# The order of the passes in products with stationary weights

## The chip, the cores and the metric

The kernel runs on one core of a Trainium2 chip. The metric is the device time of one execution in microseconds (us), the median over several runs. The core's TensorE multiplies a stationary operand of 128 x 128, loaded by one instruction (a weight load), with a moving operand of up to 512 columns that streams through it in another (a matmul, here called a pass). Sums are kept in PSUM, eight banks of 512 float32 columns per partition. VectorE (DVE), ScalarE (ACT) and GpSimd (POOL) do the elementwise work, and SyncE (SP) issues the loads.

## The reference

Two blocks run one after the other on 256 tokens of width 2048. The first has an even layer (short convolution, a state-space part, memory attention) and an odd layer (latent attention, memory attention), the second a retention layer and an MLP. Nearly all arithmetic lies in products of activations with large weights:

```python
def even_layer(x, mem_n, norm_w, w_in, ...):
    h = rms_norm(x, norm_w)
    proj = h @ w_in
    sc_b, sc_c, sc_v, sc_z, ssd_z, ssd_xbc, ssd_dt, mq, mz = _split(proj, EVEN_SPLITS)
    ...
    return x + jnp.concatenate([y_a, y_b, y_m], axis=-1) @ w_out

def odd_layer(x, mem_n, positions, norm_w, w_in, ...):
    h = rms_norm(x, norm_w)
    proj = h @ w_in
    c_q, c_kv, k_r, z_c, mq, mz = _split(proj, ODD_SPLITS)
    ...
    return x + jnp.concatenate([y_c, y_m], axis=-1) @ w_out

def squared_relu_mlp(h, w_up, w_down):
    return jnp.square(jax.nn.relu(h @ w_up)) @ w_down
```

The retention layer has the same form: an input product that gives queries, keys, values and gates, and an output product.

## The kernel before

Each product is cut into jobs. A job is one block of output columns of one weight, summed over the whole inner dimension in tiles of 128 (k tiles). PLAN lists the jobs in the order in which they run. A job is worked off in pieces of one to four k tiles (subs). For each piece SyncE loads float32 weights into a `raw` tile. ScalarE rounds them to a high part and VectorE computes the low part (value minus high part); both lie in one tile called `w` (`split_to`, `emit_split`, line 187 and line 165 in the profile). Activations are kept in the same two parts. One product of values becomes three products of parts: high by high, high by low, low by high. `emit_mm` issues them; every matmul goes through the helper `mm`, so that all have line 180. The sums of a job stand in a PSUM tile `g` of two banks; there are two such tiles.

`run_stream` sets the order by hand: for each piece it issues the splits up to two pieces ahead, the loads beyond them, then the piece's matmuls, and then steps the waiting tasks (evacuation of finished jobs, transposes, attention, normalisation), whose small matmuls fall between two pieces.

There are three kinds of jobs:

- **Kind A** (`lay_a`): the weights are stationary and the activations move, so the output is transposed. A job covers 256 output columns as two neighbouring tiles of 128, with tile 0 in bank 0 and tile 1 in bank 1. For each tile and k tile there are two passes. The first has the high weights stationary and 512 moving columns: the high and the low part of 256 tokens side by side. The second has the low weights stationary and 256 moving columns: the high part of the tokens. The profile calls them `g<-h,w` and `g<-mem,w`. Line 287 later adds the two halves of the bank.
- **Kind A3** (`lay_uq`, `lay_ukv`): weights stationary, three passes of 256 columns into one region (`g<-cq,w`, `g<-ck,w`).
- **Kind B** (`lay_b`): the activations are stationary and up to 512 weight columns move; three passes for the first 128 tokens into bank 0, then three for the second 128 into bank 1 (`g<-w,h`, `g<-w,y`, `g<-w,yr`, `g<-w,hid`, `g<-w,mem`).

PLAN holds 100 jobs of kind A. Each has 16 k tiles and two tiles: 3,200 pairs of one 512-column and one 256-column pass.

Of the kernel before, what the change touches and what calls it, by code (L numbers as in the profile page):

```python
# [118 lines left out]
def block_kernel(ctx, tc, a, out):  # L119
# [14 lines left out]
    def nm(s):  # L134
        serial[0] += 1
        return f"{s}_{serial[0]}"
# [42 lines left out]
    def mm(o, l, r, start, stop=True):  # L179
        nc.tensor.matmul(o, l, r, start=start, stop=stop, skip_group_check=True)  # L180
# [171 lines left out]
    def emit_mm(m, only=None):  # L352
        s = subs[m]
        job = s.job
        if s.first and job.ps is None:
            job.ps = psg.tile([128, 2, 512], F32, tag="g", name=nm("g"))
        hv_, lv_ = splits[m]
        for k in range(s.n):
            kt = s.k0 + s.s0 + k
            xh, xl, xb = job.x.hi(kt), job.x.lo(kt), job.x.both(kt)  # L360
            for kind, dst, (c0, c1), bk, t in job.layout(job.ps):
                if only is not None and t != only:
                    continue
                wh, wl = hv_[:, k, c0:c1], lv_[:, k, c0:c1]
                if kind == "A":
                    trio = ((dst, wh, xb), (dst[:, 0:256], wl, xh))
                elif kind == "A3":
                    trio = ((dst, wh, xh), (dst, wh, xl), (dst, wl, xh))
                else:
                    sh, sl = xh[:, t * 128:t * 128 + 128], xl[:, t * 128:t * 128 + 128]  # L370
                    trio = ((dst, sh, wh), (dst, sh, wl), (dst, sl, wh))
                for d, l, r in trio:
                    mm(d, l, r, start=bk not in job.started, stop=False)
                    job.started.add(bk)

    def spawn(gen):
        tasks.append(gen)
# [8 lines left out]
    def run_stream():  # L386
# [15 lines left out]
        for m, s in enumerate(subs):  # L402
            if s.first and s.job.key in hooks:
                hooks[s.job.key]()
            while at["split"] < n and at["split"] <= m + (min(AHEAD, m) if m < n - 4 else 3):
                dma_to(at["split"])
                emit_split(at["split"])
                at["split"] += 1
            dma_to(max(min(at["split"] + 3, m + 3), 6))
            drive(lambda: all(k in s.job.x.done for k in range(s.k0 + s.s0, s.k0 + s.s0 + s.n)))  # L410
            if m < n - 2:
                emit_mm(m)
                del splits[m]
                if s.last:
                    spawn(s.job.post(s.job.ps))
                step_tasks()

        for t in range(2):
            for m in (n - 2, n - 1):
                emit_mm(m, only=t)  # L420
            final_rows(subs[-1].job.ps, t)
# [1007 lines left out]
    for entry in PLAN:  # L1429
        key = entry[0]  # L1430
        kind, rest = key[0], key[1:]
# [115 lines left out]
```

## Time and profile before

| | |
|---|---|
| median of 3 runs | 2640.96 us (2640.96 to 2641.23) |
| the profiled execution's own time | 2640.79 us |
| its span, first to last instruction | 2639.0 us |
| PE (matmuls) busy | 2621.6 us, 99% of the span, 14,160 passes |
| PEld (weight loads) busy | 2272.8 us, 86%, 14,160 loads |
| DVE, ACT, POOL busy | 62%, 49%, 5% |
| TensorE's granted clock, mean | 0.999 |

Busy time is the time in which at least one instruction of an engine runs by its record. Matmul records overlap each other, so the busy share of PE says that it was never idle, and not how fast it went. How fast is read from how many passes fall into a stretch. A window's count includes each pass of which any part lies in it.

### The profile page before, as it was taken

The numbers are of one execution on the slowest core, as the hardware profiler recorded it, in microseconds if no ns is written. First come the engines' busy times: TensorE is split into PE (matmuls) and PEld (weight loads), VectorE is DVE, ScalarE is ACT, GpSimd is POOL, SyncE is SP. The second block draws the span as 40 slices with busy tenths as digits, with TensorE's granted clock in tenths as the row PEclk, the third lists the DMA queues.
The fourth block names the chain that finished last, engine by engine and source line by source line (L and its number), as shares of the span: only waits on it lengthen the run. The fifth ranks groups of instructions, "written<-read, shape, count | busy, mean of one in ns | idle before, by whom it ended". The sixth has DMA issues, their size and how long they took to land.

```text
span 2639.0 us, 34784 instructions
## 1 busy us (share of the span) xinstructions
PE 2621.6 (99%) x14160; PEld 2272.8 (86%) x14160; DVE 1643.1 (62%) x2067; ACT 1298.8 (49%) x1772; POOL 140.6 (5%) x104
## 2 busy tenths in 40 slices
PE   9999999999999999999999999999999999999998
PEld 7998888888899999888888888888888888888886
DVE  7657787656545887657565556565656545555554
ACT  6566555544445675545444444444455434534543
POOL 4100232000000000000000000000000000000000
PEclk9999999999999999999999999999999999999999
DMA  7454444565545434455444554554555555555553
GB/s 278 169 192 170 160 160 160 192 219 198 185 156 197 159 138 180 176 191 215 179 176 182 190 195 179 180 198 173 189 186 195 195 192 189 191 193 190 191 209 142
DMA packets 74833, 488.87 MB, mean 185 GB/s; under 512 B 8880, under 2 KB 10672, under 8 KB 20656
## 3 DMA queue, kind: packets, MB, share of 16 engines
q1 hardware_dynamic: 74096, 486.11, 51.2%
q8 instruction: 111, 1.82, 0.3%
q10 hardware_dynamic: 576, 0.53, 0.1%
q14 instruction: 50, 0.41, 0.0%
HBM read 484.51 MB, written 2.10 MB: 184 GB/s over the span
## 4 chain that ended last, share of the span: by engine, by line
PE 96%; DVE 1%; ACT 1%; DMA 1%; POOL 1%; issue 0%; POOLq 0%; ACTq 0%; DVEq 0%; SPq 0%
PE g L180 91%; PE tr L436 1%; PE ro L180 1%; PE at.s L180 1%; DVE w L165 0%; PE rs L180 0%; ACT w L187 0%; POOL xsq L487 0%; DMA raw<-in_mem_v_dram 0%; PE at.o L180 0%; PE yd L180 0%; DMA raw<-in_mem_k_dram 0%; PE seg L180 0%; DVE xbc L174 0%; PE ma.o L180 0%
## 5 line engine op out<-in xcount | busy, mean ns | idle before, releaser
L165 DVE TENSOR_TENSOR w<-raw,w 128x1024 fp32r<-128x1024 f32 (+4 forms) x929 | 1116.4, 1212 | 818.8 <-ACT w L187 817.2
L187 ACT CAST w<-raw 128x1024 fp32r<-128x1024 f32 (+4 forms) x929 | 936.3, 1026 | 652.0 <-PE g L180 639.9
L180 PE MATMUL g<-h,w 128*128 128x512 f32 (+1 forms) x6144 | 1077.5, 336 | 1.0 <-DVE qx L165 1.0
L180 PEld LDWEIGHTS g<-h,w 128*128 128x128 f32 x6144 | 935.0, 188 | 125.6 <-issue 2.0
L180 PE MATMUL g<-w,h 128*128 128x512 f32 (+3 forms) x2208 | 460.8, 368 | 0.0
L180 PEld LDWEIGHTS g<-w,h 128*128 128x128 f32 x2208 | 391.9, 188 | 59.4
L180 PE MATMUL g<-w,hid 128*128 128x512 f32 x1536 | 349.0, 389 | 0.8 <-DVE x L174 0.8
L180 PEld LDWEIGHTS g<-w,hid 128*128 128x128 f32 x1536 | 288.1, 188 | 61.0 <-DVE x L174 1.3
L180 PE MATMUL g<-w,y 128*128 128x512 f32 x1152 | 264.5, 390 | 0.0
L180 PEld LDWEIGHTS g<-w,y 128*128 128x128 f32 x1152 | 215.2, 188 | 44.7 <-ACT y L187 0.4
L287 ACT COPY low<-g 128x512 f32<-128x512 f32 x100 | 58.6, 586 | 337.0 <-PE g L180 337.0
L180 PE MATMUL g<-w,yr 128*128 128x512 f32 x768 | 176.2, 390 | 0.0
L180 PEld LDWEIGHTS g<-w,yr 128*128 128x128 f32 x768 | 143.7, 188 | 29.6
L165 DVE TENSOR_TENSOR x<-x,g 128x512 f32<-128x512 f32 x48 | 30.8, 684 | 68.0 <-PE g L180 68.0
L165 DVE TENSOR_TENSOR blk<-g,low 128x512 f32<-128x512 f32 x100 | 68.3, 683 | 0.4 <-PE g L180 0.4
L1327 POOL TENSOR_TENSOR s<-s,om 128x1 f32<-128x1 f32 x16 | 22.6, 1411 | 598.6 <-DVE s L169 598.6
L180 PE MATMUL g<-cq,w 128*128 128x256 f32 x432 | 54.3, 282 | 0.0
L465 POOL TENSOR_TENSOR stat<-s,om 128x2 f32<-128x2 f32 x7 | 10.0, 1435 | 820.9 <-DVE s L171 820.9
L180 PEld LDWEIGHTS g<-cq,w 128*128 128x128 f32 x432 | 52.1, 189 | 0.1
L180 PE MATMUL g<-w,mem 128*128 128x512 f32 x192 | 46.7, 397 | 2.6 <-ACT w L187 0.8
L180 PEld LDWEIGHTS g<-w,mem 128*128 128x128 f32 x192 | 35.2, 188 | 13.1 <-DVE mem L174 3.0
L177 ACT ACT_TABLE_LOAD x28 | 35.9, 1283 | 20.4 <-PE pre L180 10.4
(267 smaller groups left out, 1461.0 us busy)
## 6 DMA issues: line engine op xcount, KB each, us to landing
raw<-in_w_in_dram SPq DMA_DIRECT2D x96, 1024.0 KB, 4.8
raw<-in_ret_w_in_dram SPq DMA_DIRECT2D x96, 1024.0 KB, 4.8
raw<-in_mlp_w_up_dram SPq DMA_DIRECT2D x64, 1024.0 KB, 4.8
raw<-in_mlp_w_down_dram SPq DMA_DIRECT2D x64, 1024.0 KB, 4.8
raw<-in_w_out_dram SPq DMA_DIRECT2D x48, 1024.0 KB, 4.8
raw<-in_ret_w_out_dram SPq DMA_DIRECT2D x32, 1024.0 KB, 4.8
raw<-in_w_in_dram SPq DMA_DIRECT2D x12, 704.0 KB, 4.0
raw<-in_mem_k_dram SPq DMA_DIRECT2D x8, 1024.0 KB, 4.9
```

What stands on the lines that cost most here:

```text
L165: nc.vector.tensor_tensor(o, x, y, op)
L177: nc.scalar.activation(o, x, f, **kw)
L180: nc.tensor.matmul(o, l, r, start=start, stop=stop, skip_group_check=True)
L187: nc.scalar.copy(hi, x)
L287: nc.scalar.copy(low, ps[:, :, 256:512])
L436: nc.tensor.transpose(ps[:, i, t * 128:(t + 1) * 128], src(t, kp + i), ident)
L465: nc.gpsimd.tensor_tensor(dst, v, mhalf[:, 0:ncols], ALU.pow)
L1327: nc.gpsimd.tensor_tensor(r, vv, mhalf[:, 0:1], ALU.pow)
```

## The change

Within one k tile of a job of kind A, the four passes were issued tile by tile: 512 columns and 256 columns of tile 0, then 512 and 256 columns of tile 1. Now both 512-column passes come first (tile 0, tile 1) and then both 256-column passes (tile 0, tile 1). The instructions are the same in number and operands; only their order differs, and that of the weight loads with them: high 0, low 0, high 1, low 1 becomes high 0, high 1, low 0, low 1. Consecutive passes now go to different banks. Kinds A3 and B keep their order.

```diff
@@ emit_mm
             xh, xl, xb = job.x.hi(kt), job.x.lo(kt), job.x.both(kt)
+            groups = []
             for kind, dst, (c0, c1), bk, t in job.layout(job.ps):
...
-                for d, l, r in trio:
-                    mm(d, l, r, start=bk not in job.started, stop=False)
-                    job.started.add(bk)
+                groups.append((kind, bk, trio))
+            order = []
+            while groups:
+                pair = [groups.pop(0)]
+                if pair[0][0] == "A" and groups and groups[0][0] == "A" and groups[0][1] != pair[0][1]:
+                    pair.append(groups.pop(0))
+                for i in range(max(len(g[2]) for g in pair)):
+                    order += [(g[1], g[2][i]) for g in pair if i < len(g[2])]
+            for bk, (d, l, r) in order:
+                mm(d, l, r, start=bk not in job.started, stop=False)
+                job.started.add(bk)
```

## Rows read from the trace of the kernel before

**Rows 1.** The page: the span, the engines' busy time, the clock in 40 slices.
```profile
span 2639.0 us, 34784 instructions
...
PE 2621.6 (99%) x14160; PEld 2272.8 (86%) x14160; DVE 1643.1 (62%) x2067; ACT 1298.8 (49%) x1772; POOL 140.6 (5%) x104
...
PEclk9999999999999999999999999999999999999999
```

**Rows 2.** The page: the chain that ended last, by engine and line.
```profile
PE 96%; DVE 1%; ACT 1%; DMA 1%; POOL 1%; issue 0%; POOLq 0%; ACTq 0%; DVEq 0%; SPq 0%
PE g L180 91%; PE tr L436 1%; PE ro L180 1%; PE at.s L180 1%; DVE w L165 0%; PE rs L180 0%; ACT w L187 0%; POOL xsq L487 0%; DMA raw<-in_mem_v_dram 0%; PE at.o L180 0%; PE yd L180 0%; DMA raw<-in_mem_k_dram 0%; PE seg L180 0%; DVE xbc L174 0%; PE ma.o L180 0%
```

**Rows 3.** Matmul groups by shape, whole span: count, busy us, mean ns of one.
```profile
L180 PE MATMUL g<-h,w 128*128 128x512 f32 x3072 | 1066.7, 392 | 1.0 <-DVE qx L165 1.0
L180 PE MATMUL g<-h,w 128*128 128x256 f32 x3072 | 856.2, 279 | 0.0
...
L180 PE MATMUL g<-mem,w 128*128 128x512 f32 x128 | 44.5, 393 | 0.0
L180 PE MATMUL g<-mem,w 128*128 128x256 f32 x128 | 35.7, 279 | 0.0
```

**Rows 4.** PE on tile g by stretch: length, busy (count of passes), clock, DMA share, GB/s.
```profile
502.00:588.00 86.00, 86.00 (x497) 1.00 0.58 202
1351.00:1371.00 20.00, 20.00 (x119) 1.00 0.51 189
1524.00:1556.00 32.00, 32.00 (x186) 1.00 0.51 189
1708.00:1738.00 30.00, 30.00 (x175) 1.00 0.49 177
1935.00:2055.00 120.00, 120.00 (x708) 1.00 0.53 187
2195.00:2295.00 100.00, 100.00 (x579) 1.00 0.53 189
2421.00:2517.00 96.00, 96.00 (x555) 1.00 0.55 196
2065.00:2185.00 120.00, 120.00 (x531) 1.00 0.56 200
```

**Rows 5.** Matmul groups by shape, 1935 to 2055 us.
```profile
L180 PE MATMUL g<-h,w 128*128 128x512 f32 x354 | 120.4, 389 | 0.0
L180 PE MATMUL g<-h,w 128*128 128x256 f32 x354 | 97.7, 276 | 0.0
```

**Rows 6.** The same, 2195 to 2295 us.
```profile
L180 PE MATMUL g<-h,w 128*128 128x512 f32 x290 | 100.6, 392 | 0.0
L180 PE MATMUL g<-h,w 128*128 128x256 f32 x289 | 80.9, 280 | 0.0
```

**Rows 7.** The same, 2065 to 2185 us (a chain of 512-column passes of kind B).
```profile
L180 PE MATMUL g<-w,hid 128*128 128x512 f32 x531 | 120.5, 389 | 0.0
```

**Rows 8.** The same, 854.1 to 858.2 us (a chain of 256-column passes of kind A3).
```profile
L180 PE MATMUL g<-cq,w 128*128 128x256 f32 x37 | 4.5, 281 | 0.0
```

**Rows 9.** The same, 169.05 to 169.5 us (256-column passes of memory attention).
```profile
L180 PE MATMUL ma.s<-mkp,mqp 128*128 128x256 f32 x5 | 0.8, 283 | 0.0
```

**Rows 10.** The same, 2189.45 to 2189.75 us (first passes of kind A behind a chain of B).
```profile
L180 PE MATMUL g<-h,w 128*128 128x512 f32 x2 | 0.7, 394 | 0.0
L180 PE MATMUL g<-h,w 128*128 128x256 f32 x1 | 0.3, 283 | 0.0
```

**Rows 11.** Weight loads of kind A, whole span: mean ns of one.
```profile
L180 PEld LDWEIGHTS g<-h,w 128*128 128x128 f32 x6144 | 935.0, 188 | 125.6 <-issue 2.0
```

**Rows 12.** What PE waited for, longest first: us in total, times, longest.
```profile
PE ma.t L545 <- DVE p L169: 1.4, 1, 1.4
PE fs L180 <- POOL xsq L495: 1.3, 1, 1.3
```

**Rows 13.** All engines by stretch: PE, PEld, DVE, ACT, POOL; clock, DMA share, GB/s.
```profile
1935.00:2055.00 120.00, 120.00 (x708) 106.13 (x707) 71.47 (x75) 61.15 (x71) 1.60 (x1) 1.00 0.53 187
2195.00:2295.00 100.00, 100.00 (x579) 88.09 (x578) 57.23 (x57) 49.73 (x58) 0.00 (x0) 1.00 0.53 189
```

## The prediction

> **What bounds the kernel now.** I began with the page [rows 1]: PE is busy for 2621.6 of 2639.0 us, in every slice, at full granted clock. The chain that ended last says the same by another way: 96% of it is PE, 91% matmuls into the tile g [rows 2]. The longest wait of a matmul is 1.4 us in total [rows 12]. So PE is never short of work, and a change of order can act only through the rate at which passes follow each other. What matters is the distance from the start of one pass to the start of the next, which the duration of a pass does not give directly, as records overlap.
>
> I read that distance from counts per stretch [rows 4]. A pass is some 390 ns long, so about two more are counted than begin in a window. In 2065 to 2185 us, only 512-column passes of kind B, 529 begin in 120 us: 226.8 ns each. Their record lasts 389 ns [rows 7], so record minus distance is 162.2 ns. In 1935 to 2055 us, only pairs of kind A, 706 passes begin in 120 us: 339.9 ns a pair. In 2195 to 2295 us, the same instructions, 577 begin in 100 us: 346.6 ns a pair. The same code thus runs at two rates, each steady over long stretches, with the same clock; I call them the short and the long rhythm.
>
> The mean durations say where the 7 ns are [rows 5, 6]: 389 and 276 ns against 392 and 280 ns. In the short rhythm the 512-column pass takes 226.8 ns, as in the chain of B, and the 256-column pass 339.9 − 226.8 = 113.1 ns; record minus distance is then 276 − 113.1 = 162.9 ns. In the long rhythm both passes take 3 to 4 ns more. Two passes that differ by 256 columns differ by 113.7 ns here, so the columns themselves cost 0.444 ns each at most, and every pass has a fixed part that comes with the change of weights. How much of that part shows depends on how a weight load (188 ns by its record, [rows 11], started during the pass before) falls against the running pass. That last is an inference; the two rates are read.
>
> How often is each rhythm there? The undisturbed windows of kind A [rows 4] hold 140 us of the short one (1351 to 1371, 1935 to 2055) and 344 us of the long one (the five others at 347). That is 412 and 993 pairs, 29% of them in the short rhythm, and a mean of 344.7 ns a pair. Over all 3,200 pairs, with the small matmuls of other tasks in between, the groups give (392 − 162.2) + (279 − 162.9) = 345.9 ns [rows 3], 1,107 us or 42% of the span. The 1.2 ns of difference are interruptions, which the change leaves where they are.
>
> **The change, part by part.** Nothing is removed or added: 6,400 passes and 6,400 loads of kind A stay, kinds A3 and B are issued as before, and no DMA, no split and no queue is touched. Within a piece only the order differs, so the same semaphores are waited for. The low weights are needed by the third pass rather than by the second, about 0.1 us later; they were not late (no wait above 1.4 us), so this is worth nothing. The bank of tile 0 gets its last pass one pass later than before, and the evacuation waits for the whole job anyway.
>
> What changes is the neighbourhood of each pass. Four passes (a quartet) were 512, 256, 512, 256 and become 512, 512, 256, 256. There are 1,600 quartets. Before, one took 2 × 344.7 = 689.4 ns undisturbed. The new one has two transitions that the trace shows only in chains of equal passes:
>
> - 512 after 512 with new weights: 226.8 ns [rows 7].
> - 256 after 256 with new weights: in the chain of A3, 281 − 162.9 = 118.1 ns [rows 8]; in memory attention, 283 − 162.9 = 120.1 ns [rows 9].
>
> The transitions 512 to 256 and 256 to 512 inside a steady pattern are known only from the old order, in its two rhythms. I price each pass by the chain of its own kind: 2 × 226.8 + 2 × 118.1 = 689.8 ns. Against 689.4 that is 0.4 ns more, times 1,600 quartets 0.6 us. The profiled execution took 2640.79 us on its own clock (its span and 1.8 us around it), 0.17 us below the median of the three runs, so the sum gives 2641.4 us, and 2641.6 beside the median.
>
> The bounds come from the nearest rows. Lowest: the new order settles wholly in the short rhythm, each 512 at 226.8 and each 256 at 113.1, 679.8 ns a quartet: 9.6 × 1,600 = 15.4 us less. Highest of all steady patterns: 256 at the 120.1 of memory attention, 693.8 ns: 4.4 × 1,600 = 7.0 us more. I take the chain of A3 between them, because its weights come from the same tile with the same offsets as those of kind A. Above both lies the first moment after a change of pattern: the first passes of kind A behind a chain of B take 394 and 283 ns [rows 10], 231.8 and 120.1 by distance. If the new order never got beyond that, a quartet would be 703.8 ns, 23.0 us more.
>
> The other engines neither gain nor stop this: in stretches of kind A, DVE is busy 57 to 60% and ACT 50 to 51%, DMA 53% [rows 13], so that they could feed a PE that is 1.4% quicker there.
>
> One rule of the Trainium skill bears on the sum. The row first: a load lasts 188 ns by its record, and starts during the pass before [rows 11]. "TensorE: Matmul & The Clock Gate" (Part 2, the steps) states that the next weights are loaded while the current pass streams, into a background buffer, in a time that goes with the columns of the weights, by its figure 128 / 1.2 = 107 ns. By that rule each pass hides one load in either order and a quartet costs the same: the sum would be zero, by my rows 0.6 us.
>
> A second rule speaks against the change. The row first: the clock is full in all 40 slices, in kind B too, where the bank changes after every third pass, and in kind A, where it changes after every second [rows 1]. The same page ("A second HAM failure mode") states that cycling through PSUM banks each iteration made PE idle briefly, so often that its clock fell between its two levels; by that rule the new order, which changes bank with every pass, could lose clock in 42% of the span. What it would cost is the fourth rival below.
>
> **The rivals.** 0.2% of the time, 5.3 us, is about what a measurement of this kernel can tell from no change; that is 3.3 ns a quartet.
>
> - *The new order locks into the short rhythm* (faster). For it: there the 512 already takes its chain's 226.8, and a 256 can take 113.1 [rows 5]. Against it: no chain of 256-column passes in the trace runs below 118.1 [rows 8, 9]. Wholly in it: 2640.8 − 15.4 = 2625.4 us; it counts as faster when a quartet comes below 686.1 ns, that is when at least one of the two 256-column passes gets most of the 5 ns.
> - *Two short passes in a row find the load late* (slower). A 512-column pass leaves the following load ample time, a 256-column pass hardly any. In the old order no short pass followed another; in the new one it happens in each quartet, and a lead won under the long passes may be spent by the first short one. Place: the second 256 and the 512 behind it. Price: 120.1 ns for each short pass [rows 9], or the long rhythm throughout, 2 × 346.6 = 693.2: 6.1 to 7.0 us more, 2647 to 2648 us. It decides from 692.7 ns a quartet. For it: the chains of short passes come no nearer to 113.1 than 118.1 [rows 8], and 71% of the undisturbed pairs are in the long rhythm already. Against it: the old mean is so near this end that little is left to lose.
> - *The pattern never settles* (slower). Changing the neighbour every second pass keeps each pass in the condition of the first ones after a boundary [rows 10]: up to 2664 us. Against it: the old order changes its neighbour with every pass and settles all the same [rows 4].
> - *The clock falls* in stretches of kind A. At half of it each of the 768 columns of a pair would cost another 0.444 ns at most: up to 341 ns × 3,200, about 1.1 ms. Against it stands every slice of the clock row; chance 1%.
>
> That the change does not do what it says can be left out: the order of issue is written out by hand.
>
> **How the numbers follow.** No measurable change 0.43 (quartet between 686.1 and 692.7 ns, the chain prices or a mixture of the rhythms like before); short rhythm for the larger part 0.25; short passes late 0.22; never settled 0.09; clock 0.01. So faster 0.25, same 0.43, slower 0.32. The time is that of the likeliest, 2641.6 us. The range must reach into both neighbours: down to 2627, nearly the short rhythm throughout, and up to 2652, beyond the highest steady pattern by a fifth of the unsettled one. Left out are most of the unsettled cases, the clock, and the last us or two of the short rhythm, together some 0.1 to 0.15. The likeliest case's own range is 2636 to 2647.
>
> **What would show it right or wrong.** In the changed kernel the counts in long stretches of kind A give the quartet: 100 us hold 580 passes at 689.8 ns, 588 at 679.8, 577 at 693.8. The records of 512 columns should be 389 ns on average, those of 256 columns 281. A mean of 276 for the short ones is the lock into the short rhythm; 283 is the late load; 392 and more for the long ones is the pattern that does not settle. The stretch of kind B, 226.8 ns a pass, must be the same, the clock row full, and the waits of PE no longer than 1.4 us. The prediction is wrong if the time moves by more than 5.3 us, and its reasoning is wrong, even at an unchanged time, if the two rhythms come at quite different prices.

## The result and the profile after

The changed kernel takes 2661.61 us (median of 4 runs, 2661.38 to 2663.26) against 2641.10 us before: 20.5 us slower, ratio 1.008, 95% interval 1.0067 to 1.0092. Executions of one kernel lay within 1.9 us of each other, the noise by which the single runs below are to be read. The forecast of 2641.6 us and its range up to 2652 were wrong. The time is that of the rival which had been given 9%, "the pattern never settles", up to 2664 us. Whether its reason was right as well is what the experiments had to tell.

The page of the changed kernel, its span, the engines and the clock, answers to [rows 1]:

```profile
span 2660.0 us, 34784 instructions
...
PE 2642.9 (99%) x14160; PEld 2280.4 (86%) x14160; DVE 1644.1 (62%) x2067; ACT 1299.2 (49%) x1772; POOL 139.5 (5%) x104
...
PEclk9999999999999999999999999999999999999999
```

The span grew by 21.0 us, PE's busy time by 21.3; the clock is full in every slice, the counts are the same. What PE waited for, longest first (us in total, times, longest), answers to [rows 12]:

```profile
PE fs L180 <- POOL xsq L504: 1.5, 1, 1.5
PE ma.t L554 <- DVE p L169: 1.2, 1, 1.2
```

No wait has appeared: the longest is 1.5 us where it was 1.4. Where did 20.5 us go? The matmul groups by shape over the whole span answer to [rows 3]:

```profile
L180 PE MATMUL g<-h,w 128*128 128x512 f32 x3072 | 970.4, 397 | 1.0 <-DVE qx L165 1.0
L180 PE MATMUL g<-h,w 128*128 128x256 f32 x3072 | 610.8, 281 | 0.0
```

The busy column invites a wrong reading: it fell from 1066.7 to 970.4 and from 856.2 to 610.8 us, and yet the kernel is slower. Passes of one shape now follow each other, their records overlap, and overlapped time counts once. The mean of one is the column to read: 392 became 397 ns for the long passes, 279 became 281 for the short ones. Times 3,200 each that is 16 and 6 us, 22 us with both rounded to whole nanoseconds.

Counts of PE on tile g by stretch (length, busy, count, clock, DMA share, GB/s), two stretches of kind A and then one of kind B, answer to [rows 4]:

```profile
1960.00:2060.00 100.00, 100.00 (x572) 1.00 0.53 187
2215.00:2315.00 100.00, 100.00 (x572) 1.00 0.51 182
2085.00:2185.00 100.00, 100.00 (x443) 1.00 0.55 195
```

570 passes begin in 100 us, in the first stretch (which had the short rhythm before) as in the second (which had the long one). A quartet takes 400 / 570 us = 701.8 ns on average in both. Against the undisturbed mean of 689.4 ns before, that is 12.4 ns × 1,600 = 19.8 us: nearly the whole loss lies between passes of kind A. The trace also records the start of every single pass, which the views here only average. Added up from each start to the next, the passes of kind A took 1110.6 us before and take 1131.1 us now, 20.5 of the 21.0 us by which the span grew. The chain of kind B has 441 passes in 100 us, 226.8 ns each, as before. In the second stretch of kind A the groups of kind A are, against [rows 6]:

```profile
L180 PE MATMUL g<-h,w 128*128 128x512 f32 x286 | 90.2, 396 | 0.0
L180 PE MATMUL g<-h,w 128*128 128x256 f32 x286 | 56.9, 280 | 0.0
```

With the same subtraction as in the prediction: 396 − 162.2 = 233.8 ns for a long pass, 280 − 162.9 = 117.1 ns for a short one; 2 × (233.8 + 117.1) = 701.8 ns, the count's own number. Most of the loss lies in the long passes: of the 20.5 us by the starts, 16.7 are theirs and 3.8 those of the short ones.

### The profile page after: what moved, and what is told of

Read it like the earlier page. It is cut to its first block, busy times and chain, and to the rows that moved or that the text cites. A ratio compares the mean times of both kernels' runs of the same rounds, so it can differ in the third digit from the quotient of the medians.

```text
span 2660.0 us, 34784 instructions
## 1 busy us (share of the span) xinstructions
PE 2642.9 (99%) x14160; PEld 2280.4 (86%) x14160; DVE 1644.1 (62%) x2067; ACT 1299.2 (49%) x1772; POOL 139.5 (5%) x104
## 4 chain that ended last, share of the span: by engine, by line
PE 96%; DVE 1%; ACT 1%; DMA 1%; POOL 1%; issue 0%; POOLq 0%; ACTq 0%; DVEq 0%; SPq 0%
PE g L180 91%; PE tr L445 1%; PE ro L180 1%; PE at.s L180 1%; DVE w L165 0%; PE rs L180 0%; ACT w L187 0%; DMA raw<-in_mem_v_dram 0%; PE at.o L180 0%; DMA raw<-in_mem_k_dram 0%; PE yd L180 0%; POOL xsq L496 0%; PE seg L180 0%; DVE xbc L174 0%; DMA mem<-in_mem_dram 0%
## 5 line engine op out<-in xcount | busy, mean ns | idle before, releaser
L180 PE MATMUL g<-h,w 128*128 128x512 f32 (+1 forms) x6144 | 1097.1, 339 | 1.0 <-DVE qx L165 1.0
L180 PEld LDWEIGHTS g<-h,w 128*128 128x128 f32 x6144 | 946.9, 188 | 143.4 <-issue 2.1
```

## The experiments

Three theories stood at the start. Theory 1: the order of lengths costs the time (what the surviving rival said). Theory 2: a pass into another bank than the one before it costs more. Theory 3: high weights loaded after high and low after low cost the time. The kernel before, run on the same chip beside each set, took 2640.8 to 2641.7 us. Each experiment was run once, unless an interval is given.

**Banks.** The first run alternates the lengths as before and lets the second tile's short pass come early; the four passes go to banks 0, 1, 1, 0.

```diff
+            if groups[0][0] == "A":
+                (_, b0, p0), (_, b1, p1) = groups
+                order = [(b0, p0[0]), (b1, p1[1]), (b1, p1[0]), (b0, p0[1])]
...
```

> The order of passes is 512 columns into bank 0, 256 into bank 1, 512 into bank 1, 256 into bank 0. Long and short passes alternate as before the change; the bank changes at two of four passes, and never between the pair of one tile's passes as it did; the high and low weights alternate too. Theory 1 (the order of lengths costs the time): 2641 us, within 8 us, since long and short alternate. Theory 2 (a pass that goes to another bank than the pass before it costs more): about half of the loss or more, 2650 to 2662 us. Theory 3 (high weights loaded after high, low after low, cost the time): 2641 us, since they alternate.

Measured: 2640.81 us. Theory 2 has no support, though the number of bank changes is that of before. The second run settles it: the lengths of the changed kernel, all four passes into one bank.

```diff
+        quads = {}
...
+                if kind == "A":
+                    quads.setdefault((k // 2, bk), []).append(trio)
+                    continue
...
+        for (_, bk), two in quads.items():
+            for i in range(2):
+                for trio in two:
+                    mm(*trio[i], start=bk not in job.started, stop=False)
+                    job.started.add(bk)
```

> Two k tiles of one tile are taken together: 512, 512, 256, 256 columns, all four into one bank, then the same for the other tile. Lengths in the order of the changed kernel, bank changes only once in four passes. Theory 1 (order of lengths): 2661 us, a quartet of about 702 ns with long passes at 233 to 236. Theory 2 (banks): 2641 us or less. Theory 3 (high after high, low after low): 2661 us.

Measured: 2662.78 us. Its groups over the whole span:

```profile
L180 PE MATMUL g<-h,w 128*128 128x512 f32 x3072 | 971.2, 397 | 1.0 <-DVE qx L165 1.0
L180 PE MATMUL g<-h,w 128*128 128x256 f32 x3072 | 611.6, 281 | 0.0
```

397 and 281 ns, as in the changed kernel, with a quarter of its bank changes. Theory 2 falls.

**Lengths against loads.** Which weights a pass loads and how many columns it has can be separated: two runs cross the two orders. In both, the second and the third pass of a quartet multiply by each other's weights, so the work is the same and the result is not.

```diff
# lengths and banks of before, loads of the changed kernel
+                seq = [(b0, p0[0]), (b0, p0[1]), (b1, p1[0]), (b1, p1[1])]
+                ws = [p0[0][1], p1[0][1], p0[1][1], p1[1][1]]
# lengths and banks of the changed kernel, loads of before
+                seq = [(b0, p0[0]), (b1, p1[0]), (b0, p0[1]), (b1, p1[1])]
+                ws = [p0[0][1], p0[1][1], p1[0][1], p1[1][1]]
# both
+                order = [(bk, (p[0], l, p[2])) for (bk, p), l in zip(seq, ws)]
```

> Lengths and banks of the kernel before (512, 256, 512, 256; bank 0, 0, 1, 1), but the stationary weights in the order of the changed kernel (high 0, high 1, low 0, low 1), so that the second and the third pass multiply with the wrong weights: a part of the products is changed, the amount of work is not. Theory 1 (order of lengths): 2641 us, within 8 us. Theory 2 (banks): 2641 us. Theory 3 (order of the loads): 2661 us.

> Lengths and banks of the changed kernel (512, 512, 256, 256; bank 0, 1, 0, 1), but the stationary weights in the order of before (high 0, low 0, high 1, low 1), so that the second and the third pass multiply with the wrong weights: a part of the products is changed, the amount of work is not. Theory 1 (order of lengths): 2661 us. Theory 2 (banks): 2661 us. Theory 3 (order of the loads): 2641 us, within 8 us.

| | loads high, low, high, low | loads high, high, low, low |
|---|---|---|
| lengths 512, 256, 512, 256 | 2640.9 us (before) | 2658.24 us |
| lengths 512, 512, 256, 256 | 2664.60 us | 2661.61 us (changed) |

The groups of the first (upper right) and of the second (lower left), whole span:

```profile
L180 PE MATMUL g<-h,w 128*128 128x512 f32 x3072 | 1083.1, 395 | 1.0 <-DVE qx L165 1.0
L180 PE MATMUL g<-h,w 128*128 128x256 f32 x3072 | 864.0, 281 | 0.0
```

```profile
L180 PE MATMUL g<-h,w 128*128 128x512 f32 x3072 | 967.5, 396 | 1.0 <-DVE qx L165 1.0
L180 PE MATMUL g<-h,w 128*128 128x256 f32 x3072 | 614.9, 281 | 0.0
```

Theories 1 and 3 both fall, each by one corner: restoring the loads does not help while the lengths are new, and restoring the lengths does not while the loads are new. In both runs the long passes last 395 to 396 ns and the short ones 281, against 392 and 279. Only one of the four corners is quick. Nor is it that the lengths change too often. A run with all eight long passes of a piece first and then all eight short ones:

```diff
+        long, short = [], []
...
+                if kind == "A":
+                    long.append((bk, trio[0]))
+                    short.append((bk, trio[1]))
+                    continue
...
+        for bk, (d, l, r) in long + short:
+            mm(d, l, r, start=bk not in job.started, stop=False)
+            job.started.add(bk)
```

> All eight long passes of a piece of four k tiles run first, then all eight short ones, at the offsets of before. Theory 1, in the form that a change of length costs the long passes after it: 1,600 quartets have one change from short to long each, here every fourth has one, so that a quarter to a half of the loss is left, 2646 to 2652 us. Theory 4: long passes now have high loads under them, short passes low loads, as in the changed kernel, and the loss stays: 2655 us or more.

Measured: 2664.74 us. Its groups over the whole span:

```profile
L180 PE MATMUL g<-h,w 128*128 128x512 f32 x3072 | 784.4, 397 | 1.0 <-DVE qx L165 1.0
L180 PE MATMUL g<-h,w 128*128 128x256 f32 x3072 | 425.6, 281 | 0.0
```

With one change from long to short in sixteen passes, the long passes are as slow as with one in four.

**Where the loads start.** What the four corners share is the tile w: its high parts start at float32 element 1048 and its low parts at 12, that is 8 and 12 beyond a multiple of 16. Theory 4: the distance between passes depends on where the data of the next load start, so that an order and the starts have to fit each other. The edit is one line in each case; the passes of kind A3 use the same tile and move with it.

```diff
-PHASES = {"A": (1024 + 24, 12), "B": (1024 + 8, 8)}
+PHASES = {"A": (1024 + 32, 0), "B": (1024 + 8, 8)}
```

> The order of the kernel before; in the tile w of kind A the high parts start at element 1056 and the low parts at element 0, both at a multiple of 16 elements, where they started at 1048 and 12 (8 and 12 beyond such a multiple). Theory 4 (the time between passes depends on where the start of the next load lies, so that order and offsets have to fit each other): the time moves by more than 8 us, most likely up towards 2655 to 2665 us. Theory 1 (the order of lengths alone): 2641 us.

> The order of the changed kernel with the same aligned starts, 1056 and 0. With equal starts the order of high and low loads can make no difference, only the order of lengths can. Theory 4: within 4 us of the old order with aligned starts. Theory 1: 20 us above the old order with aligned starts, near 2661 us.

Measured: 2653.59 us for the old order, 2648.74 us for the new one. The old order lost 12 us and the new one gained 13; with equal starts, the new order is the quicker of the two by 4.9 us, where Theory 4 had said within 4. Counts of the new order (first fence) and of the old one (second), aligned, in two stretches of kind A:

```profile
1960.00:2050.00 90.00, 90.00 (x522) 1.00 0.53 187
2220.00:2300.00 80.00, 80.00 (x464) 1.00 0.52 187
```

```profile
1960.00:2050.00 90.00, 90.00 (x517) 1.00 0.53 189
2220.00:2300.00 80.00, 80.00 (x464) 1.00 0.55 194
```

By (count − 2) per length, a quartet of the new order takes 692.3 and 692.6 ns, one of the old order 699.0 and 692.6 ns. The old order shows its short rhythm in neither stretch: one runs at 699.0 ns, a rate that it did not have in these stretches at 8 and 12. The other, and the new order in both, run at about the rate of the old long rhythm (2 × 346.6 = 693.2 ns). That the rates move with the starts is Theory 4, and Theory 1 falls a second time: it had no reason for either move.

Is it the difference of the two starts (4a), or the place of each (4b)?

> The order of the changed kernel, high and low parts both starting 8 elements beyond a multiple of 16 (1048 and 8). Theory 4a (only the difference of the two starts matters, equal starts are good for this order): 2648.7 us, within 2 us, as with both starts at a multiple. Theory 4b (the place of each start against the moving columns matters by itself): more than 4 us away from 2648.7.

> The order of the changed kernel, high parts at a multiple of 16 elements (1040), low parts 8 elements beyond one (8). Theory 4a: the difference of 8 is larger than the 4 of the changed kernel, so 2661 us or more. Theory 4b: no sign is given; a time below 2648.7 would show that unequal starts can be the better ones in this order too.

> The order of the changed kernel, high parts 8 elements beyond a multiple of 16 (1048), low parts at a multiple (0). Theory 4a: the same as with 0 and 8, within 3 us, 2661 us or more. Theory 4b: differs from it by more than 4 us.

> The order of the kernel before, both starts 8 elements beyond a multiple of 16 (1048 and 8). Theory 4a: 2653.6 us, within 2 us, as with both at a multiple. Theory 4b: more than 4 us away from that.

Measured: 2676.83, 2662.32, 2656.41 and 2643.14 us. Both starts at 8 instead of 0 cost the new order 28 us more and the old one 10 us less, with no difference between the two starts in either case. 4a had its number for 0 and 8 (2661 us or more) and missed the other three. So the place of the starts matters, and not only their difference: 4b. That it is their place against the moving columns is not shown, as those were never moved. The groups of the new order with both at 8, whole span, and the counts of the old order with both at 8:

```profile
L180 PE MATMUL g<-h,w 128*128 128x512 f32 x3072 | 977.3, 398 | 1.0 <-DVE qx L165 1.0
L180 PE MATMUL g<-h,w 128*128 128x256 f32 x3072 | 623.0, 283 | 0.0
```

```profile
1960.00:2050.00 90.00, 90.00 (x516) 1.00 0.53 189
2220.00:2300.00 80.00, 80.00 (x473) 1.00 0.53 185
```

The old order shows its two rhythms here as well, 350.2 and 339.7 ns a pair, with the stretches exchanged against [rows 4].

The starts of single passes show what the counts average. In ns from each start to the next, in order of issue (for the old order, where long and short alternate, both of a kind are alike):

| order, starts of high and low parts | 512 columns | 256 columns | quartet |
|---|---|---|---|
| old, 8 and 12, 1935 to 2055 us | 227 | 113 | 680 |
| old, 8 and 12, 2195 to 2295 us | 229 | 117.6 | 693.3 |
| new, 8 and 12, 1960 to 2060 us | 230 to 236, 231 to 236 | 113 to 118, 117 to 120 | 697 to 707 in turn, mean 702.2 |
| new, 0 and 0, 1960 to 2050 us | 231, 229 | 118, 115 | 693.3 |
| new, 8 and 8, 2220 to 2300 us | 238, 233 | 124, 118 | 713.3 |

In four of these rows each quartet is like the last within a nanosecond or so: the pattern has settled. In the changed kernel it has not: the quartets go round (707, 697, 703, 706, 698, 702 and so on).

**Does the new order have starts that suit it?**

> The order of the changed kernel, both starts 12 elements beyond a multiple of 16 (1052 and 12). Theory 5a (the new order, too, has starts that suit it, and they can be found): one of the four runs of this set comes to 2641 us or below. Theory 5b (the new order keeps a loss at any starts): all four stay at or above 2646 us. If the time goes smoothly with the start, this one lies between 2648.7 (0) and 2676.8 (8).

> The order of the changed kernel, both starts 4 elements beyond a multiple of 16 (1044 and 4). Theories 5a and 5b as in the run with 12 and 12; if the time goes smoothly with the start, between 2648.7 and 2676.8 us.

> The order of the changed kernel, high parts at a multiple of 16 (1040), low parts 12 beyond one (12), as before. Against the changed kernel only the start of the high parts differs. If the high parts' start carries the loss, near 2648.7 us; if the low parts' does, near 2661 us.

> The order of the changed kernel, high parts at a multiple of 16 (1040), low parts 4 beyond one (4). If the high parts' start carries the loss, near 2648.7 us; if the low parts' does, somewhere between that and 2662 us.

Measured: 2667.82, 2658.44, 2663.64 and 2653.47 us. None reaches 2646, so 5b stands as far as it was tried. The times with 12 and 12 and with 4 and 4 lie between 2648.7 and 2676.8, as a smooth course would have it. With the high parts at 0, the low start at 0, 4, 8 and 12 gives 2648.7, 2653.5, 2662.3 and 2663.6 us; low at 12, the high start at 0, 8 and 12 gives 2663.6, 2661.6 and 2667.8. Up to here the low start carries the larger part. But with the low start at 8, moving the high one from 0 to 8 takes the time from 2662.3 to 2676.8 us, so neither part carries the loss alone.

One more pair, the two starts of before exchanged, was tried with the new order:

> The order of the changed kernel with the two offsets exchanged: the high parts start 12 elements beyond a multiple of 16 (element 1052), the low parts 8 beyond one (element 24). Theory 4: the time moves by more than 4 us from 2661 us, either way. Theory 1: 2661 us.

It took 9412.66 us, because the granted clock fell after 740 us (last section); as a time it says nothing. Up to there the clock was full. Its groups in 520 to 570 us:

```profile
L180 PE MATMUL g<-h,w 128*128 128x512 f32 x143 | 45.0, 395 | 0.0
L180 PE MATMUL g<-h,w 128*128 128x256 f32 x143 | 28.7, 282 | 0.0
```

2 × (395 − 162.2 + 282 − 162.9) = 703.8 ns a quartet, 2 ns from the changed kernel's 701.8. Times 1,600 that would be 3 us, below the 4 us that Theory 4 had wanted to see. A change of start can happen to cost next to nothing.

**Is there a quicker version near the old one?** These two were run several times, 4 and 10, beside the kernel before:

> The order of the kernel before, high parts starting 8 elements beyond a multiple of 16 (1048), low parts 10 beyond one (10), between the two known times of 2643.1 (8 and 8) and 2641 us (8 and 12). Theory 6a (the old order changes slowly with the low start): 2640 to 2644 us. Theory 6b (each start has its own rhythms): outside of that, and if below 2636 us, a version that beats both kernels.

> The order of the kernel before, both starts 12 elements beyond a multiple of 16 (1052 and 12); against the kernel before only the high parts' start differs. Theory 6a: within 4 us of 2641 us. Theory 6b: outside of that.

Measured: 2657.08 us (ratio 1.0061, interval 1.0044 to 1.0078) and 2647.66 us (1.0025, 1.0016 to 1.0034). Both are slower than before, so 6b, but no version beats both kernels. Of the five pairs tried with the old order, 8 and 12 is the lowest, 8 and 8 lies 2 us above it, about the spread of runs, and 8 and 10, between the two, costs 14 to 16 us more than they do.

## Why the prediction was wrong

- **What bounds the kernel** was right: PE's rate between passes and nothing else. No new wait, no other engine and no clock appears in the profile after, the chain of kind B kept its 226.8 ns, and outside kind A the span grew by only 0.5 us.
- **The step that failed** is "I price each pass by the chain of its own kind: 2 × 226.8 + 2 × 118.1 = 689.8 ns". The term 2 × 118.1 was right within 2 ns (2 × 117.1). The term 2 × 226.8 was mis-sized: the long passes take 2 × 233.8. That is 14.0 ns a quartet, 22.4 us in all, of which the short ones give 3.2 us back. The chain of B has other operands: there the weights are the moving side and the activations are loaded, from other starts. The experiments show that the distance between the passes of kind A depends on where the loads' data start: the same new order goes from 2648.7 to 2676.8 us by the starts alone. A price read beside other loads did not carry over. Why the chain of B has just 226.8 ns was not tested.
- **The fixed part of a pass**, said to come with the change of weights, does not follow from 226.8 and 113.1 ns: that is 0.443 and 0.442 ns a column, which leaves nothing over. (With the 118.1 ns of the A3 chain for the short pass, 9 ns would be left.) The mean of 344.7 ns a pair took the rate of one long window for all five, whose counts give 347.1; nothing hangs on it, since the single starts of all undisturbed pairs give 344.6.
- **"The highest of all steady patterns"**, 693.8 ns, failed with the price. It was the highest among the patterns in the trace, not a bound of the chip. A quartet takes 701.8 ns on average here, and a steady one takes 713.3 with both starts at 8.
- **The rival that never settles** had the right size, since it took both prices, 231.8 and 120.1 ns, from passes of kind A behind passes of kind B [rows 10], the only rows with a long pass of kind A right after another long pass. Its sign, long records of 392 ns and more, came too (397). Its reason was only half right. By the single starts the old order does settle behind that boundary, its long passes going 233, 234, 231 and then 229 ns, and the changed kernel's quartets do not come to one length. But that is not what costs the time: with both starts at 8 the new order is settled and slower still (713.3 ns), at 0 it is settled and quick (693.3), and with eight equal passes in a row the loss stayed.
- **The late load behind short passes** did not come at its price: 117.1 ns on average, under both chains' prices. In the place that it named, the second short pass takes 118.6 ns against 115.8 for the first, and the long pass behind it 233.4, less than the next one's 234.5.
- **Lock into the short rhythm**: no stretch of the changed kernel runs in it, 572 passes in both.
- **The two rules.** Banks: the clock row is full after the change too, and four passes in one bank cost as much as four in alternating banks (2662.8 and 2661.6 us). What the Trainium skill states in "TensorE: Matmul & The Clock Gate" (A second HAM failure mode) had no bearing here. Hidden loads: if each pass hid its load at no cost in either order, as the prediction took the rule, a quartet would have kept its 689.4 ns. It takes 701.8, and moving nothing but the starts of the loaded data changed the time of the same instructions by 28 us. The load's own record stays at 187 to 188 ns meanwhile. The same page of the Trainium skill (Part 2, the steps) also says that the weights have a read port of their own, so that loading them takes nothing from the running pass; no run here shows a read, so this is neither borne out nor refuted. Of the starts tried, 10 is the only one that is not a multiple of four elements, and the old order was 14 to 16 us slower there than at 8 and at 12. The Trainium skill gives lines of 16 bytes in SBUF, four elements here ("Advanced Engine Details and Errata", SBUF Cachelines), and says nothing there of where an operand starts. One such start is no proof, and starts on such lines differ by as much.

What stays open is the mechanism. That the starts and the order act together is shown, for kind A only: the passes of kind A3, whose loads were moved too, kept their time, 74.4 to 75.3 us from start to start in every run at full clock. The writes of the splits, whose places moved too, are not the cause: a quartet of the changed kernel that no other task interrupts takes 702.1 ns while ScalarE or VectorE writes such a tile and 702.0 ns while neither does; with both starts at 8 it is 712.4 ns either way. That a load's reads and the running pass's reads get in each other's way in SBUF, depending on how they fall in time, would explain it and is only argued: nothing in the trace shows a read. Why one stretch of the old order falls into the short rhythm and another into the long one is open as well. In the aligned runs the high parts start at element 1056, in the other runs called 0 at 1040: whether a distance of 16 elements matters was not tried. Nor were other starts than the nine pairs tried with the new order, the tenth being the one whose clock fell.

## What to carry to other kernels

In this kernel a price for a pass held only with the loads beside which it was read; where the matmul engine never waits, the order of passes and the start addresses of their stationary operands are one setting, to be tried together. When an order is changed in a kernel whose operands lie at odd offsets, vary the offsets as well before judging the order: with aligned starts the verdict here had the other sign, 4.9 us for the new order, though both were then slower than the kernel before. And read the distance between passes from counts in a window, for a group's busy time can fall by more than a quarter while the kernel gets slower.

## What the runs showed of the hardware unexpectedly

- The same 14,160 passes and loads, with no wait, take between 2641 and 2677 us by nothing but the order of a piece's passes and the start of the weights in SBUF, in steps of a few elements. A long pass of 512 columns took 226.8 ns at best and 398 − 162.2 = 235.8 ns on average with both starts at 8 in the new order. Settled quartets were read at 680.0, 693.3 and 713.3 ns.
- In one run the clock fell to levels below both of the known ones. The rows of PE on that run around the fall (length, busy, count, clock, DMA share, GB/s):

```profile
700.00:740.00 40.00, 40.00 (x182) 1.00 0.54 185
740.00:760.00 20.00, 20.00 (x56) 0.61 0.33 118
760.00:800.00 40.00, 40.00 (x40) 0.16 0.06 20
...
5720.00:5800.00 80.00, 80.00 (x103) 0.26 0.12 42
```

PE had not been idle for as much as 0.1 us since 250 us when the clock fell to 0.16 and later to 0.26 of full, until the end. The lower of its two known levels, 1.2 GHz, would be 0.50. The other 17 experiments kept the full clock. Nothing in the trace names a cause.
